# Rotary tables with a longer due time, the decay polynomial in eight late tasks, squares on four regions, the instruction order made anew

## The chip, the cores and the metric

The kernel runs on one core of a Trainium2 chip. The metric is the time of one execution on the device, in microseconds: 1812.16 us is the median of three runs of the kernel before (1810.64 to 1813.06).

## What is computed

One layer of a diffusion backbone on 256 latent and 256 context tokens of width 4096, all in fp32. Modulated RMS-normalised rows go through one wide input projection; its columns are attention queries, keys, values and gate, and the recurrent branch's input and gate. What the change touches is the rotary position code of queries and keys, the RMS norm of each head, and the decay of the recurrence, which needs a softplus of `lam`:

```
mod = silu(c) @ w_ada + b_ada                       # shift, scale, gate
h   = rmsnorm(x, norm_w) * (1 + scale) + shift      # latent rows; context rows likewise
q, k, v, ga, xl, gl = split(h @ w_in)
q, k = rmsnorm per head; q, k = apply_rope(q, k)    # latent rows only
att  = softmax(q k_all) v_all                       # 16 query heads, 4 key heads
u    = short_conv(xl)
r, i = sigmoid(u @ wa + ba), sigmoid(u @ wx + bx)   # block-diagonal
log_a = -8 * r * softplus(-lam)                     # the decay
a, b  = exp(log_a), sqrt(-expm1(2 log_a)) * i * u   # scanned in both directions
out = x + gate * (concat(rmsnorm(att) * silu(ga), rmsnorm(lru) * silu(gl)) @ w_out)
```

## The kernel before, in words

The products run on TensorE in three passes, a weight and an activation each being split into a high part (ScalarE, line 654 for weights) and a low part (VectorE, line 658). Weights come in 512 KB loads from the SP queue (line 305) into six slots; a slot is free again when its low part is made, and the next load is issued then. There are three slots for high parts and three for low parts.

Stage 1 goes over the 32 blocks of 128 input rows in groups of 1, 1, 2, 2, 2 and then 4 blocks. For each group the modulation (w_ada) is computed first, partly on TensorE (line 493), partly on VectorE (481, 483), the activations are scaled, turned and split (605, 615, 616, 625), and then the columns of k, v and the four parts of xl are multiplied (755 to 757). The four tiles of tokens of one column block fill the four PSUM banks `pm`; VectorE adds each to its sum in SBUF (775), which frees the bank for the next column block. Groups go through the six column blocks forwards and backwards in turn, so the last group begins with k. Stage 2 makes the queries (941 to 943), the attention and, beside it, the recurrence; stage 3 the gates (965 to 967); stage 4 the output projection. The gate columns of w_ada are multiplied on VectorE (871, 873) wherever there is room from the end of stage 1 on.

The order of all instructions is made by a planner that runs when the kernel is built (`Plan`, lines 91 to 212). Each `add` gives a task: a function that emits instructions, its costs by engine (P TensorE, A ScalarE, D VectorE, S a transfer issued by GpSimd), the tasks it depends on, a position `pos` (in us of TensorE work) that decides among tasks that can start within 0.10 us of each other, a position `nb` of the main products before which it may not be ordered, and the slots that it takes and gives back. The planner always takes the task that can start earliest. It keeps one clock `dma` for all transfers: a load arrives 1.44 us or more after that clock, and no sooner than 2.2 us after its slot came free (lines 129 to 135); an S task puts its own cost on the same clock:

```
t.end = self.dma = max(self.dma, t.start + 1.3) + t.ops[0][1]   # 205
t.end += 0.9                                                    # 207
```

The order in which tasks are taken is the order of the instructions in each engine's queue; the costs have no other effect.

What the change touches: `decay` (414 to 432) turns `lam` into `lp`, the factor of the decay that the recurrence needs; it is called in one task with `params(1, 2)` at line 830, in the third group. `rope_tasks` (434 to 455) gives two tasks: `load` writes one element on VectorE (440), behind which GpSimd issues eleven transfers (442, 447, 448), and `mul` multiplies the table by the norm's weight (451). It is called for the keys at line 831 and for the queries at line 1417; the keys are normed, rotated and turned in `key_tasks` (1007 to 1045), the queries in `q_head_tasks` (1051 to 1083), and the recurrence's first task depends on the queries' table too (1322). `sum_squares` (979 to 984) squares four heads on ScalarE, each with an accumulator read. `norm_cols` (975 to 977) is a square root on ScalarE and a reciprocal on VectorE.

Of the kernel before, what the change touches and what calls it, by code (L numbers as in the profile page):

```python
# [76 lines left out]
def pe(n, k=1):  # L77
    return k * n / 2400


def mm(n, k=1):

    return k * (n / 2400 + 0.0136)
# [132 lines left out]
def kernel(  # L216
# [197 lines left out]
    def decay():  # L414

        tl = slot("td", [128, 4, 32])
        V.tensor_scalar_mul(tl[:, 0], lam, -1.0)
        V.tensor_tensor(out=tl[:, 1], in0=tl[:, 0], in1=lam, op=ALU.max)
        S.activation(tl[:, 1], tl[:, 1], AF.Exp, scale=-1.0)
        V.tensor_scalar_add(tl[:, 2], tl[:, 1], 2.0)  # L420
        V.reciprocal(out=tl[:, 2], in_=tl[:, 2])
        V.tensor_tensor(out=tl[:, 1], in0=tl[:, 1], in1=tl[:, 2], op=ALU.mult)
        V.tensor_tensor(out=tl[:, 2], in0=tl[:, 1], in1=tl[:, 1], op=ALU.mult)
        V.memset(tl[:, 3], 1.0 / 17.0)
        for k in (15, 13, 11, 9, 7, 5, 3, 1):
            V.tensor_tensor(out=tl[:, 3], in0=tl[:, 3], in1=tl[:, 2], op=ALU.mult)
            V.tensor_scalar_add(tl[:, 3], tl[:, 3], 1.0 / k)
        V.tensor_tensor(out=tl[:, 3], in0=tl[:, 3], in1=tl[:, 1], op=ALU.mult)
        V.tensor_scalar(out=tl[:, 0], in0=tl[:, 0], scalar1=0.0, scalar2=4.0, op0=ALU.max, op1=ALU.mult)
        V.scalar_tensor_tensor(out=lp[:, 0], in0=tl[:, 3], scalar=8.0, in1=tl[:, 0], op0=ALU.mult, op1=ALU.add)  # L430
        V.tensor_scalar_mul(lp[:, 1], lp[:, 0], -1.0)
        drop(tl)

    def rope_tasks(w, pos, after):
# [19 lines left out]
        a = add(load, [("S", 2.0)], after, pos, nb=pos - 20, acq=["u"])  # L454
# [3 lines left out]
    def mod_tasks(k0, nk, out_, p0, p1, nb, cl, on_v=(0, 0)):  # L458
# [58 lines left out]
        for part, col0 in enumerate((128 * k0, D + 128 * k0)):  # L517
# [3 lines left out]
            while k < KT:  # L521
# [8 lines left out]
                else:  # L530
                    m = max(4, step)
                    todo.append(("P", lambda *ws, part=part, k=k: on_tensor(*ws, part=part, k=k), [("P", m // 4 * (pe(4 * n) + 0.2))],
# [139 lines left out]
    def piece(fn, cost, pos, deps, last_of=None, acq=(), rel=()):  # L672


        def run():
            fn()
            if last_of is not None:
                drop(units[last_of]["hi"], units[last_of]["lo"])
            drop(*(x for f in rel for x in f()))

        t = add(run, [("P", cost + 0.025)], [main[0]] + deps, pos, acq=acq, rel=["h4"] * (2 * len(rel)) + (["hi", "lo"] if last_of is not None else []))
        t.main = True
        main[0] = t
        return t
# [145 lines left out]
    t = add(lambda: (params(1, 2), decay()), [("P", 0.3), ("D", 1.0), ("A", 0.3, "exp"), ("D", 2.5)], [p_late], starts[2] - 2, nb=starts[1] + 1, acq=["pe"], rel=["xin", "pe"])  # L830
    k_rope = rope_tasks(k_norm_w, starts[-2] + 8, [t])
# [29 lines left out]
    def gate_tasks(j, prev):  # L861
# [28 lines left out]
        a = add(sums, [("P", 0.43)], [prev], pos, acq=["pe"], rel=["ga"])  # L890
# [315 lines left out]
    def lru_tasks(n, pos, span, prev):  # L1206
# [114 lines left out]
        ld = add(load, [("S", 1.0)], [spilled[n // 4], prev.get("ld")], at(-0.5), nb=at(-0.8), acq=["wg", "xin"])  # L1321
# [9 lines left out]
        for r in range(2):  # L1331
            w = at(0.2 + 0.15 * r)
            ts = []
            for z in range(2):
                a = add(lambda r=r, z=z: gate(r, z), [("P", pe(1536))], [parts], w + 0.06 * span * z, acq=["pe"], rel=["hi", "lo", "lg"] if r and z else [])
# [197 lines left out]
```

## Time and profile before

| | us |
|---|---|
| median of three runs | 1812.16 |
| profiled execution | 1807.69 |
| its span, first to last instruction | 1805.5 |
| TensorE busy (matmul) | 1736.0 |
| VectorE busy | 1383.2 |
| ScalarE busy | 865.0 |
| mean granted TensorE clock | 0.991 |

Times in the profile are counted from the first instruction of the span. PE is TensorE, PEld its weight loads, DVE VectorE, ACT ScalarE, POOL GpSimd, SP SyncE. A wait is written as the instruction that waited, an arrow, and what came last before it could start. Tiles are named as in the program, without buffer numbers: `a` is a sum of stage 1, `hi` and `lo` the parts of a weight, `h` those of the activations, `raw` a load's slot, `rope` and `u` the rotary table and its second factor, `td` the scratch of the polynomial, `ta` and `tp` other scratch.

### The profile page before, as it was taken

The page shows a single profiled execution, that of the slowest core. Times are in us where ns is not written, and L with a number is a line of the kernel's source. Part 1 is how long each engine was busy: PE and PEld are TensorE (multiplying, and loading weights), DVE is VectorE, ACT ScalarE, POOL GpSimd, SP SyncE. Part 2 cuts the span into 40 slices and gives each one's busy share as a digit, 9 for nine tenths or more (in the row PEclk, how much of TensorE's full clock was granted, in tenths as well). Part 3 has the DMA queues.
Part 4 walks back from the last instruction along what each step waited for, and adds up shares of the span by engine and source line. Part 5 has one row for each costly group of instructions (what it writes and reads, how often), then busy time and mean ns, then how long its engine had stood idle before and what let it go on. Part 6 is the DMA issues. An engine that isn't in the chain of part 4 may idle for free.

```text
span 1805.5 us, 25645 instructions
## 1 busy us (share of the span) xinstructions
PE 1736.0 (96%) x9693; PEld 1388.1 (77%) x9693; DVE 1383.2 (77%) x1965; ACT 865.0 (48%) x1282; POOL 67.8 (4%) x111
## 2 busy tenths in 40 slices
PE   3999999999999989999999999999999999999998
PEld 2556667676767767777777889999999988888887
DVE  1278989797978866457789877997996998686864
ACT  5522232232313233347887776868667643333332
POOL 1000000000000010100000000000000000000000
PEclk9999999999999989999999999999999999999999
DMA  9999987869696974863446636875885699898983
GB/s 322 329 303 325 324 302 266 311 227 342 222 345 224 334 198 145 234 195 126 156 148 233 195 110 214 263 232 177 282 268 161 221 322 343 278 334 275 334 273 116
DMA packets 286331, 451.80 MB, mean 250 GB/s; under 512 B 15136, under 2 KB 122512, under 8 KB 285696
## 3 DMA queue, kind: packets, MB, share of 16 engines
q1 hardware_dynamic: 279392, 428.43, 71.1%
q0 software_dynamic: 6816, 21.74, 4.2%
q8 instruction: 76, 1.25, 0.3%
q14 instruction: 47, 0.39, 0.1%
HBM read 441.72 MB, written 8.39 MB: 249 GB/s over the span
## 4 chain that ended last, share of the span: by engine, by line
PE 73%; DVE 14%; DMA 5%; ACT 4%; issue 3%; SPq 1%; POOL 0%; DVEq 0%; ACTq 0%; POOLq 0%
PE pm L755 8%; PE pm L942 8%; PE pm L943 8%; PE pm L941 8%; PE pm L757 7%; PE pm L756 7%; PE pm L965 6%; PE pm L966 6%; PE pm L967 6%; DVE lo L658 4%; DMA raw<-in_w_ada_dram 3%; PE pt L493 2%; PE po L493 2%; DVE ga L873 2%; DVE a L775 1%
## 5 line engine op out<-in xcount | busy, mean ns | idle before, releaser
L654 ACT CAST hi<-raw 128x1024 fp32r<-128x1024 f32 x416 | 436.0, 1049 | 713.2 <-PE pm L757 269.2
L658 DVE TENSOR_TENSOR lo<-raw,hi 128x1024 fp32r<-128x1024 f32 x416 | 506.4, 1220 | 191.3 <-ACT hi L654 189.4
L755 PE MATMUL pm<-hi,h 128*128 128x512 f32 x768 | 318.0, 414 | 16.4 <-DVE a L775 10.9
L941 PE MATMUL pm<-hi,h 128*128 128x512 f32 x768 | 310.2, 404 | 0.0
L942 PE MATMUL pm<-lo,h 128*128 128x512 f32 x768 | 300.1, 391 | 8.0 <-DVE lo L658 8.0
L757 PE MATMUL pm<-hi,h 128*128 128x512 f32 x768 | 302.9, 394 | 3.7 <-DVE h L625 3.7
L756 PE MATMUL pm<-lo,h 128*128 128x512 f32 x768 | 302.8, 394 | 0.8 <-DVE lo L658 0.8
L943 PE MATMUL pm<-hi,h 128*128 128x512 f32 x768 | 300.1, 391 | 0.0
L965 PE MATMUL pm<-h,hi 128*128 128x256 f32 x1024 | 293.7, 287 | 0.0
L967 PE MATMUL pm<-h,lo 128*128 128x256 f32 x1024 | 289.9, 283 | 0.3 <-DVE lo L658 0.3
L966 PE MATMUL pm<-h,hi 128*128 128x256 f32 x1024 | 289.7, 283 | 0.0
L755 PEld LDWEIGHTS pm<-hi,h 128*128 128x128 f32 x768 | 145.6, 190 | 112.6 <-issue 41.4
L965 PEld LDWEIGHTS pm<-h,hi 128*128 128x128 f32 x1024 | 196.2, 192 | 2.2 <-issue 1.2
L966 PEld LDWEIGHTS pm<-h,hi 128*128 128x128 f32 x1024 | 196.3, 192 | 2.1 <-issue 1.2
L967 PEld LDWEIGHTS pm<-h,lo 128*128 128x128 f32 x1024 | 196.2, 192 | 0.5 <-DVE lo L658 0.5
L873 DVE SCALAR_TENSOR_TENSOR ga<-raw,sc,ga 128x512 f32<-128x512 f32 x248 | 185.9, 750 | 10.6 <-DMA raw<-in_w_ada_dram 5.0
L942 PEld LDWEIGHTS pm<-lo,h 128*128 128x128 f32 x768 | 144.8, 189 | 41.2 <-DVE lo L658 9.5
L757 PEld LDWEIGHTS pm<-hi,h 128*128 128x128 f32 x768 | 146.0, 190 | 36.5 <-DVE h L625 4.1
L941 PEld LDWEIGHTS pm<-hi,h 128*128 128x128 f32 x768 | 144.6, 188 | 31.8 <-issue 3.6
L943 PEld LDWEIGHTS pm<-hi,h 128*128 128x128 f32 x768 | 144.4, 188 | 30.6
L756 PEld LDWEIGHTS pm<-lo,h 128*128 128x128 f32 x768 | 146.2, 190 | 27.0 <-DVE lo L658 1.3
L775 DVE TENSOR_TENSOR a<-pm,a 128x512 f32<-128x512 f32 x202 | 132.6, 683 | 32.4 <-PE pm L757 32.1
(193 smaller groups left out, 1710.4 us busy)
## 6 DMA issues: line engine op xcount, KB each, us to landing
raw<-in_w_ada_dram SPq DMA_DIRECT2D x384, 512.0 KB, 5.6
raw<-in_w_in_dram SPq DMA_DIRECT2D x288, 512.0 KB, 4.6
raw<-in_w_out_dram SPq DMA_DIRECT2D x128, 512.0 KB, 5.2
h<-in_x_dram SPq DMA_DIRECT2D x8, 512.0 KB, 9.2
h<-in_ctx_dram SPq DMA_DIRECT2D x8, 512.0 KB, 10.6
xl_d<-a POOLq DMA_DIRECT2D x4, 1024.0 KB, 6.5
xin<-xl_d POOLq DMA_DIRECT2D x16, 256.0 KB, 4.9
a<-in_x_dram POOLq DMA_DIRECT2D x8, 512.0 KB, 7.1
```

Of the source, the lines that this page charges most:

```text
L654: S.copy(d["hi"], raw)
L658: V.tensor_tensor(out=d["lo"], in0=d["raw"], in1=d["hi"].bitcast(F32), op=ALU.subtract)
L755: T.matmul(ps[s, t], hi, wh, start=f, stop=False)
L756: T.matmul(ps[s, t], hi, wl, start=False, stop=False)
L757: T.matmul(ps[s, t], lo, wh, start=False, stop=e)
L873: V.scalar_tensor_tensor(out=d["acc"], in0=w[:, i], scalar=s_, in1=d["acc"], op0=ALU.mult, op1=ALU.add)
L941: T.matmul(ps[t], hi, wh, start=f, stop=False)
L942: T.matmul(ps[t], hi, wl, start=False, stop=False)
L943: T.matmul(ps[t], lo, wh, start=False, stop=e)
L965: T.matmul(o, wh, hi, start=f, stop=False, skip_group_check=True)
L966: T.matmul(o, wh, lo, start=False, stop=False, skip_group_check=True)
L967: T.matmul(o, wl, hi, start=False, stop=e, skip_group_check=True)
```

## The change

The rotary load's cost goes from 2.0 to 15.0 and its `pos` from that of the product to 20 ahead of it; its `nb` is as before, 20 ahead of the product. The keys' call moves from 8 to 28 behind the start of the last group, so that the load may be ordered from 8 behind that start on, and not from 12 ahead of it. The queries' call is as before. `decay` becomes eight tasks in a chain, of which the first may be ordered from 28 behind the start of the last group on; its scratch is a `tp` slot and no longer `td`, and the recurrence's loads wait for the last of the eight in the plan. The squares of four heads go to four regions of one `ta` tile, where each took and gave back the same region. Planned costs of several task kinds are changed (main products, modulation products, squares, gate sums, the recurrence's gates), and the order of the whole kernel is made from them.

```diff
 def mm(n, k=1):
-    return k * (n / 2400 + 0.0136)
+    return k * (n / 2400 + 0.0134)
...
-    def decay():
+    def decay_tasks(pos, step, after):
+        d = {}
+        def begin():
+            tl = d["tl"] = slot("tp", [128, 4, 32])
+            V.tensor_scalar_mul(tl[:, 0], lam, -1.0)
+            V.tensor_tensor(out=tl[:, 1], in0=tl[:, 0], in1=lam, op=ALU.max)
+        def expo():
+            S.activation(d["tl"][:, 1], d["tl"][:, 1], AF.Exp, scale=-1.0)
+        def ratio():
...
+        def series(ks):
+            tl = d["tl"]
+            for k in ks:
+                V.tensor_tensor(out=tl[:, 3], in0=tl[:, 3], in1=tl[:, 2], op=ALU.mult)
+                V.tensor_scalar_add(tl[:, 3], tl[:, 3], 1.0 / k)
+        def finish():
...
+        parts = [(begin, ("D", 0.35)), (expo, ("A", 0.15, "exp")), (ratio, ("D", 1.1))]
+        parts += [(lambda ks=ks: series(ks), ("D", 0.9)) for ks in ((15, 13), (11, 9), (7, 5), (3, 1))] + [(finish, ("D", 0.85))]
+        a = after
+        for i, (fn, op) in enumerate(parts):
+            a = add(fn, [op], [a], pos + step * i, nb=pos - 2 if i == 0 else None, acq=["tp"] if i == 0 else [], rel=["tp"] if fn is finish else [])
+        return a
...
-        a = add(load, [("S", 2.0)], after, pos, nb=pos - 20, acq=["u"])
+        a = add(load, [("S", 15.0)], after, pos - 20, nb=pos - 20, acq=["u"])
         return add(mul, [("D", dve(512))], [a], pos, rel=["u"])
...
-[("P", m // 4 * (pe(4 * n) + 0.2))]
+[("P", m // 4 * (pe(4 * n) + 0.145) + 0.09)]
...
-        t = add(run, [("P", cost + 0.025)], ...
+        t = add(run, [("P", cost)], ...
...
-    t = add(lambda: (params(1, 2), decay()), [("P", 0.3), ("D", 1.0), ("A", 0.3, "exp"), ("D", 2.5)], [p_late], starts[2] - 2, ...
-    k_rope = rope_tasks(k_norm_w, starts[-2] + 8, [t])
+    t = add(lambda: params(1, 2), [("P", 0.37), ("D", 0.9)], [p_late], starts[2] - 2, ...
+    k_rope = rope_tasks(k_norm_w, starts[-2] + 28, [t])
+    decayed = decay_tasks(starts[-2] + 30, 3.0, t)
...
-        a = add(sums, [("P", 0.43)], [prev], pos, acq=["pe"], rel=["ga"])
+        a = add(sums, [("P", 0.8)], [prev], pos, acq=["pe"], rel=["ga"])
...
     def sum_squares(src, ss):
+        j = slot("ta", [128, 4, 128])
         for n in range(4):
-            j = slot("ta", [128, 128])
-            S.activation(j, src[:, n], AF.Square, accum_out=ss[:, n : n + 1])
-            drop(j)
-    SUMSQ = 4 * (act(128) + 0.09)
+            S.activation(j[:, n], src[:, n], AF.Square, accum_out=ss[:, n : n + 1])
+        drop(j)
+    SUMSQ = 4 * (0.215 + 0.091)
...
-        ld = add(load, [("S", 1.0)], [spilled[n // 4], prev.get("ld")], ...
+        ld = add(load, [("S", 1.0)], [spilled[n // 4], prev.get("ld"), decayed], ...
...
-[("P", pe(1536))]
+[("P", 0.693)]
```

## Rows read from the trace of the kernel before

**Rows 1.** The page: busy us (share of the span) and instructions.
```profile
PE 1736.0 (96%) x9693; PEld 1388.1 (77%) x9693; DVE 1383.2 (77%) x1965; ACT 865.0 (48%) x1282; POOL 67.8 (4%) x111
```

**Rows 2.** Waits of PE: waiting line, releaser: us in total, times, longest.
```profile
PE pm L755 <- DVE a L775: 10.9, 4, 8.4
PE pm L942 <- DVE lo L658: 8.0, 2, 7.5
...
PE pm L757 <- DVE h L625: 3.7, 1, 3.7
...
PE pt L493 <- DMA raw<-in_w_ada_dram: 1.7, 3, 1.1
```

**Rows 3.** Windows, early groups: length, busy by engine, PEclk, DMA share, GB/s.
```profile
110.70:116.40 5.70, 5.70 (x24) 2.62 (x24) 2.97 (x6) 0.00 (x0) 0.00 (x0) 0.50 0.92 301
110.00:140.00 30.00, 29.25 (x173) 17.59 (x173) 24.54 (x48) 4.07 (x6) 0.00 (x0) 0.89 0.88 288
140.00:200.00 60.00, 58.56 (x315) 36.34 (x315) 49.22 (x81) 13.25 (x21) 0.00 (x0) 1.00 0.95 330
```

**Rows 4.** Windows, same columns: behind the two long waits, and the last group.
```profile
663.70:669.30 5.60, 5.60 (x15) 4.52 (x16) 5.37 (x9) 4.59 (x9) 0.00 (x0) 0.50 0.37 111
696.00:742.00 46.00, 44.67 (x197) 37.05 (x198) 32.86 (x51) 8.92 (x9) 1.62 (x3) 1.00 0.59 195
...
771.60:775.10 3.50, 3.48 (x10) 2.89 (x11) 2.24 (x2) 0.08 (x1) 0.50 (x1) 0.50 0.90 276
```

**Rows 5.** Timeline of DVE at the polynomial: start, us, line, op, tiles.
```profile
102.59 0.17 DVE L417 TENSOR_SCALAR td<-parT 128x32 f32<-128x32 f32 x1
...
108.98 0.18 DVE L431 TENSOR_SCALAR lp<-lp 128x32 f32<-128x32 f32 x1
...
110.21 0.76 DVE L625 TENSOR_TENSOR h<-ta,h 128x256 fp32r<-128x256 f32 x2
```

**Rows 6.** Timeline of DVE at the keys' rotary table; in brackets, idle before.
```profile
650.98 0.06 DVE L440 MEMSET rope<- 128x1 f32 x1
...
662.33 0.69 DVE L451 TENSOR_TENSOR rope<-rope,u 128x512 f32<-128x512 f32 x1 [11.28 <-DMA u<-in_shape_consts_dram]
```

**Rows 7.** Timeline of DVE in the last group's first column block.
```profile
680.43 1.23 DVE L658 TENSOR_TENSOR lo<-raw,hi 128x1024 fp32r<-128x1024 f32 x1 [4.21 <-ACT hi L654]
681.58 1.28 DVE L775 TENSOR_TENSOR a<-pm,a 128x512 f32<-128x512 f32 x2
```

**Rows 8.** Timeline of SP: issues of loads; two single ones left out.
```profile
647.46 1.50 SPq L305 DMA_DIRECT2D raw<-in_w_in_dram  x2
665.45 0.37 SPq L305 DMA_DIRECT2D raw<-in_w_ada_dram  x1
...
671.45 17.49 SPq L305 DMA_DIRECT2D raw<-in_w_in_dram  x6
```

**Rows 9.** Timeline of DVE at the queries' rotary table.
```profile
757.49 0.06 DVE L440 MEMSET rope<- 128x1 f32 x1
769.74 0.69 DVE L451 TENSOR_TENSOR rope<-rope,u 128x512 f32<-128x512 f32 x1 [12.19 <-DMA wg<-in_lru_wa_dram]
```

**Rows 10.** Timeline of ACT at the keys' squares and their root.
```profile
685.96 0.18 ACT L983 ACTIVATION_READ_ACCUMULATOR ta<-a 128x1 f32 x1
686.17 0.31 ACT L983 ACTIVATE ta<-a 128x128 f32<-128x128 f32 x1
...
693.62 1.28 ACT L976 ACT_TABLE_LOAD   x1
694.92 0.31 ACT L976 ACTIVATE ss<-ss,epsc 128x16 f32<-128x16 f32 x1
```

**Rows 11.** Timeline of ACT at the row statistics, which alternate between two slots.
```profile
41.20 0.20 ACT L392 ACTIVATION_READ_ACCUMULATOR tp<-h 128x1 f32 x1
41.30 0.63 ACT L392 ACTIVATE tp<-h 128x512 f32<-128x512 f32 x1
```

**Rows 12.** Timeline of PE behind the keys' reciprocal.
```profile
697.33 0.47 PE L755 MATMUL pm<-hi,h 128*128 128x512 f32 x1 [1.70 <-DVE a L775]
```

More of the change, by code (lines that the diff above doesn't have):

```diff
@@ L412, in params @@
             V.tensor_scalar_mul(parT[:, 1, 0:32], parT[:, 1, 0:32], 0.5)
-    def decay():
[L416 to L432, printed above, removed]
+    def decay_tasks(pos, step, after):
[8 more added lines that the diff above has]
+            tl = d["tl"]
+            V.tensor_scalar_add(tl[:, 2], tl[:, 1], 2.0)
+            V.reciprocal(out=tl[:, 2], in_=tl[:, 2])
+            V.tensor_tensor(out=tl[:, 1], in0=tl[:, 1], in1=tl[:, 2], op=ALU.mult)
+            V.tensor_tensor(out=tl[:, 2], in0=tl[:, 1], in1=tl[:, 1], op=ALU.mult)
+            V.memset(tl[:, 3], 1.0 / 17.0)
+        def series(ks):
+            tl = d["tl"]
+            for k in ks:
+                V.tensor_tensor(out=tl[:, 3], in0=tl[:, 3], in1=tl[:, 2], op=ALU.mult)
+                V.tensor_scalar_add(tl[:, 3], tl[:, 3], 1.0 / k)
+        def finish():
+            tl = d["tl"]
+            V.tensor_tensor(out=tl[:, 3], in0=tl[:, 3], in1=tl[:, 1], op=ALU.mult)
+            V.tensor_scalar(out=tl[:, 0], in0=tl[:, 0], scalar1=0.0, scalar2=4.0, op0=ALU.max, op1=ALU.mult)
+            V.scalar_tensor_tensor(out=lp[:, 0], in0=tl[:, 3], scalar=8.0, in1=tl[:, 0], op0=ALU.mult, op1=ALU.add)
+            V.tensor_scalar_mul(lp[:, 1], lp[:, 0], -1.0)
+            drop(tl)
+        parts = [(begin, ("D", 0.35)), (expo, ("A", 0.15, "exp")), (ratio, ("D", 1.1))]
[4 more added lines that the diff above has]
+        return a
@@ L679, in run @@
             drop(*(x for f in rel for x in f()))
-        t = add(run, [("P", cost + 0.025)], [main[0]] + deps, pos, acq=acq, rel=["h4"] * (2 * len(rel)) + (["hi", "lo"] if last_of is not None else []))
+        t = add(run, [("P", cost)], [main[0]] + deps, pos, acq=acq, rel=["h4"] * (2 * len(rel)) + (["hi", "lo"] if last_of is not None else []))
         t.main = True
@@ L829 @@
     p_late = add(load_params, [("S", 0.3)], [t], U1 * 0.6)
-    t = add(lambda: (params(1, 2), decay()), [("P", 0.3), ("D", 1.0), ("A", 0.3, "exp"), ("D", 2.5)], [p_late], starts[2] - 2, nb=starts[1] + 1, acq=["pe"], rel=["xin", "pe"])
-    k_rope = rope_tasks(k_norm_w, starts[-2] + 8, [t])
+    t = add(lambda: params(1, 2), [("P", 0.37), ("D", 0.9)], [p_late], starts[2] - 2, nb=starts[1] + 1, acq=["pe"], rel=["xin", "pe"])
+    k_rope = rope_tasks(k_norm_w, starts[-2] + 28, [t])
+    decayed = decay_tasks(starts[-2] + 30, 3.0, t)
     spans = {}
@@ L1319, in at @@
             return pos + span * f
-        ld = add(load, [("S", 1.0)], [spilled[n // 4], prev.get("ld")], at(-0.5), nb=at(-0.8), acq=["wg", "xin"])
+        ld = add(load, [("S", 1.0)], [spilled[n // 4], prev.get("ld"), decayed], at(-0.5), nb=at(-0.8), acq=["wg", "xin"])
         a = add(turn, [("P", 0.44)], [ld, prev.get("cv"), q_rope], at(-0.05), nb=at(-0.6), acq=["pe"], rel=["xin"])
@@ L1334, in lru_tasks @@
             for z in range(2):
-                a = add(lambda r=r, z=z: gate(r, z), [("P", pe(1536))], [parts], w + 0.06 * span * z, acq=["pe"], rel=["hi", "lo", "lg"] if r and z else [])
+                a = add(lambda r=r, z=z: gate(r, z), [("P", 0.693)], [parts], w + 0.06 * span * z, acq=["pe"], rel=["hi", "lo", "lg"] if r and z else [])
                 ts.append(add(lambda r=r, z=z: th(r, z), [("A", act(512) + 0.05, "exp")], [a] + this[:1], w + span * (0.03 + 0.06 * z),
```

2 lines of the change are left out of this document (1 added, 1 removed).

## Prediction

> **What bounds the kernel now.** I read the busy times first: TensorE works for 1736.0 of 1805.5 us [rows 1], so only the 69 us in which it stands, and the stretches in which it runs at half clock, can be won. Then I read TensorE's waits [rows 2]. Most of the rest of the 69 us is the start of the kernel, which the change does not touch. Three long waits are left: 8.4 us on an accumulation (L775), 7.5 us on a low part (L658) and 3.7 us on a remainder of the activations (L625). The windows [rows 3, 4] show that each is followed by TensorE at the lower of its two clock levels (PEclk 0.50): 5.7 us after the first in time, 5.6 and 3.5 us after the others. Work done at half clock takes twice as long, so half of each stretch is lost. The prices are 3.7 + 2.85 = 6.5 us at 107 us, 8.4 + 2.8 = 11.2 us at 655 us and 7.5 + 1.75 = 9.3 us at 764 us, 27 us in all. None of the three is TensorE's own work; in each, VectorE's queue stands still or is busy with something small while TensorE needs the next entry of it.
>
> **Part 1: the decay polynomial leaves the early groups.** Its 27 small VectorE instructions run from 102.59 to 109.16 us, 6.5 us; the remainder that TensorE waits for (L625) is queued right behind them and a low part, at 110.21 [rows 5]. That is the 3.7 us wait, and 2.85 us of half clock follow. Taken away, the low part comes 6.5 us sooner and the wait goes: at most 6.5 us. What is late next are the weight loads: there the transfers run at 330 GB/s when TensorE keeps going (140 to 200 us) and at 288 GB/s over 110 to 140 us [rows 3]. The hole is (330 - 288) x 30 / 330 = 3.8 us of transfers; TensorE cannot get further ahead than the loads do. Bounds 0 (the loads were just in time anyway) and 6.5; I take 3.8, since the windows are the row of that very resource.
>
> **Part 2: the same polynomial in the last group.** The same 6.5 us of VectorE, in eight tasks of at most 1.1 us that other work can stand between. They start 28 us of TensorE work into the last group. From 696 to 742 us VectorE is busy for 32.86 of 46 us [rows 4], so 13.1 us are free and 6.5 fit. Bounds 0 and 6.5 + 2.85 = 9.35 (all of it on the path, as at 102 us); I take 0.5, because the free time is twice what is needed. ScalarE gets an Exp between the keys' Sqrt and the first query head's Sqrt. The table load ahead of the keys' Sqrt (1.28 us at 693.62 [rows 10]) goes, since the last table before it is then a Sqrt's, and one Exp and one Sqrt load come behind it. ScalarE is busy for 8.92 of those 46 us [rows 4]: nothing, at worst 1.3 us. The Sqrt behind the load at 693.62 starts 0.02 us after that load's end [rows 10]. The Trainium skill speaks against the change here: its page "ScalarE: Activation LUTs" (What ACT_TABLE_LOAD costs, and Table sets) wants the functions of one set done together and puts a switch at about 2.66 us, 1.38 of them a drain behind the load. The row shows no such drain; by the page the worst case of this step, and with it the sum, would come out 1.4 us later.
>
> **Part 3: squares without the shared scratch.** In before each square and its accumulator read write one region; the next square starts 0.21 us after the read's start [rows 10]. The row statistics, which alternate between two slots, start 0.10 us after [rows 11]. So 0.11 us go from each of 48 squares. The 32 of the query heads lie in ScalarE's idle time. The 16 of the keys hold the Sqrt, the reciprocal behind it on VectorE, and behind that an accumulation for which TensorE waits 1.70 us at 697.33 [rows 12]. 16 x 0.11 + 1.28 for the table load = 3.0 us sooner is more than 1.70, so this wait closes: bounds 0 and 1.7, I take 1.5.
>
> **Part 4: the keys' rotary table.** Loading it is a VectorE memset (L440), eleven transfers issued by GpSimd behind it, and the product (L451) on VectorE. In before memset and product are neighbours in VectorE's queue: the product stands 11.28 us [rows 6], and all accumulations behind it with it. The change starts the transfer 20 us later than before (8 us into the last group instead of 12 us ahead of it), with a due time 13 us longer. But the planner has one clock for transfers. Line 205 puts the 15 us on that clock, every later weight load is counted from it (lines 130 to 135), and the product is due 1.05 us after it, ahead of the next load's 1.5. So nothing that needs a later load can come between memset and product; only accumulations can. And that clock runs behind: a load's slot comes free six loads before its use. The unit whose low part is at 680.43 [rows 7] was loaded by the second issue of the row at 647.46, six issues before the slot that this low part frees [rows 8]. With 2.2 + 1.44 us for the planner's load the clock stands at 652.2, and 681.6 less the 11.2 us of stall between them is 670.4: it lags by 18 us. 15 + 1.05 us do not make up for 18, so the product is due at once, or after one accumulation. At 8 us into the last group two of the first block's four accumulations are due (the row at 681.58 [rows 7]); the other two then stand behind the product. VectorE stays held for 11.3 us and TensorE again waits for a bank, about 7.7 to 8.4 us, with half clock behind it. The gain is between -1 us (block boundary hit worse) and 9.9 (all accumulations ahead, 1.3 us of wait left, no clock drop). I take 1.0, as the lag of 18 is nearest to the first.
>
> **Part 5: the queries' rotary table.** Position and start are unchanged. VectorE's memset is at 757.49 and the product waits 12.19 us [rows 9] (the name in that row is of the transfer issued behind). By the same rule only VectorE work without loads could come between, and in before there is none at that place although all of it was free to go there: the next entries are low parts [rows 2]. So the 9.3 us stay: bounds of the gain 0 and 9.3, I take 0.
>
> **Part 6: the order made anew.** Planned costs change by 0.02 to 0.37 us a task. I take 0 for it, with 2 us either way: the sum of TensorE's small waits on VectorE that such shifts move is of that size [rows 2].
>
> **Sum.** The profiled execution took 1807.69 us (span 1805.5 and 2.2 around it). 1807.69 - 3.8 + 0.5 - 1.5 - 1.0 - 0 = 1801.9 us. The median of the runs is 1812.16, 4.5 above the profiled one; so 1806.4 us.
>
> **Rivals.** A, the keys' product behind all accumulations: if the planner's clock lags by under 13 us instead of 18, the three open accumulations come first, and TensorE loses about 1.9 us there instead of 10.2: 1806.4 - 8.3 = 1798.1 us. For it: in steady state loads are used faster than in the stretch that I counted. Against: the count. B, the change does what it says, both products find their tables: 1806.4 - 10.2 - 9.3 = 1786.9 us. Against it is line 205. The Trainium skill, page "GPSIMD Engine Reference" (Specifications), adds that GpSimd shares its SBUF interfaces with VectorE instructions of two inputs; no run shown here has both at work during these transfers, and by it they would take longer under cover, not shorter. C, the loads swallow the early gain (TensorE waits for loads of w_ada in places already, 1.7 us of them on L493 alone [rows 2], and each load is as late as its slot comes free): 1806.4 + 3.8 = 1810.2 us, no change. D, slower: hold and decay now fall in one group. 11.3 + 6.5 = 17.8 us against 13.1 free. If the order puts the polynomial ahead of accumulations, VectorE falls 4.7 us behind, the 6.5 us come on the path and the clock falls once more: 4.7 + 6.5 + 2.85 - 0.5 = 13.6, 1820 us. It decides from the point at which the eight pieces, with the wait of the third for Exp, no longer find 6.5 us. Against: TensorE itself stands for most of the hold, so only some 3 us of it become arrears.
>
> **How the numbers follow.** Forecast 0.50, A 0.15, B 0.07, C 0.16, D 0.12. The forecast's own bounds are 1803 to 1810. From 1795 to 1814 only B and D are left out, 0.19. A measurement of this kernel can tell about 0.2%, 3.6 us, from no change. Below 1808.5 lie three quarters of the forecast, A and B: 0.59. Above 1815.8 lies D: 0.12. The rest is 0.29.
>
> **What would show it.** Right: no half clock between 100 and 125 us and no wait of TensorE on L625 there; a wait of the keys' product of about 10 us on VectorE in the last group with a TensorE wait of 7 to 9 us on L775 behind it; a wait of about 7.5 us on a low part at the queries' product; no wait over 1 us at the keys' reciprocal. Wrong: either product without a wait, transfers at 340 GB/s and TensorE waiting for loads from 110 us on, or a new half clock while the polynomial runs.

## The result and the profile after

| | before | after |
|---|---|---|
| median of four runs (us) | 1811.4 | 1787.31 |
| ratio, 95% interval | | 0.9865, 0.9847 to 0.9883 |
| profiled execution, its span (us) | 1807.69, 1805.5 | 1786.01, 1783.9 |
| mean granted TensorE clock | 0.991 | 0.995 |

The change takes 24.1 us away, 1.35%. The time is 19.1 us below the forecast (1806.4) and below its range. All lines of the file behind the new functions stand some 20 lower: L755 to L757 are now L776 to L778, L775 is L796, L942 is L964, L658 is L679, L493 is L514, the rotary memset and product L461 and L472.

The page's busy times after, to be read beside [rows 1]:

```profile
PE 1729.4 (97%) x9693; PEld 1387.2 (78%) x9693; DVE 1383.1 (78%) x1965; ACT 862.4 (48%) x1282; POOL 67.9 (4%) x111
```

VectorE does the same work; TensorE's busy time itself is 6.6 us shorter, with the same 9693 matmuls. Some 4 us of it are half clock, which the prediction had priced; the rest is a surprise, since it had said that only the time in which TensorE stands, and half clock, could be won.

Waits of PE after (waiting line, releaser: us in total, times, longest), beside [rows 2]:

```profile
PE po L514 <- DMA raw<-in_w_ada_dram: 24.9, 13, 18.2
PE pm L776 <- DVE a L796: 7.0, 3, 6.1
PE pm L964 <- DVE lo L679: 4.6, 2, 4.2
...
PE pm L963 <- ACT hi L675: 1.7, 1, 1.7
```

Two of the three long waits are still there, shorter: 6.1 us at the keys' table, 4.2 and 1.7 us at the queries'. The third, on a remainder of the activations, is gone. Windows after (length, busy of PE, PEld, DVE, ACT, POOL, PEclk, DMA share, GB/s), beside [rows 3, 4]:

```profile
104.00:110.00 6.00, 6.00 (x46) 3.80 (x42) 3.19 (x4) 2.66 (x5) 0.00 (x0) 1.00 1.06 353
110.00:140.00 30.00, 29.93 (x192) 18.40 (x184) 24.46 (x47) 4.57 (x5) 0.00 (x0) 1.00 0.98 318
140.00:200.00 60.00, 59.00 (x319) 37.14 (x319) 49.97 (x82) 16.98 (x28) 0.00 (x0) 1.00 0.98 339
670.10:676.90 6.80, 5.91 (x14) 4.67 (x15) 5.27 (x8) 2.54 (x10) 0.00 (x0) 0.50 0.46 141
...
686.00:732.00 46.00, 46.00 (x204) 38.09 (x203) 33.30 (x66) 12.03 (x12) 2.15 (x4) 1.00 0.65 221
...
752.00:758.85 6.85, 3.19 (x8) 2.52 (x9) 5.04 (x6) 0.85 (x1) 2.16 (x3) 0.50 0.54 182
```

In the early groups TensorE runs at full clock and almost without a hole (1.0 of 60 us in the third row). The half-clock stretches (PEclk 0.50) behind the two rotary tables remain. In the fifth row, while the polynomial runs (690.79 to 699.24), TensorE is busy for all 46 us.

Of the 21.6 us of span, the records give 15.0 to TensorE's idle time up to its last matmul (64.7 to 49.7 us), 4.4 to half clock (half of the time worked in it: 10.6 to 6.2), and 2.2 to matmuls that follow each other more closely. By place: about 1.0 at the kernel's start, where the profiled execution of before was 1 us later than those of most kernels here; 6.5 at the early polynomial; 2.2 and 1.8 at the two tables; 1.7 at the keys' reciprocal; the other 8.4 are spread over small waits of all stages. These are places, not yet causes.

### The profile page after: what moved, and what is told of

It is laid out like the page before. It is cut to its first block, busy times and chain, and to the rows that moved or that the text cites. A ratio compares the mean times of both kernels' runs of the same rounds, so it can differ in the third digit from the quotient of the medians.

```text
span 1783.9 us, 25648 instructions
## 1 busy us (share of the span) xinstructions
PE 1729.4 (97%) x9693; PEld 1387.2 (78%) x9693; DVE 1383.1 (78%) x1965; ACT 862.4 (48%) x1282; POOL 67.9 (4%) x111
## 4 chain that ended last, share of the span: by engine, by line
PE 73%; DVE 12%; DMA 7%; ACT 4%; issue 3%; SPq 1%; POOL 0%; DVEq 0%; ACTq 0%; POOLq 0%
PE pm L776 8%; PE pm L964 8%; PE pm L963 8%; PE pm L965 8%; PE pm L777 7%; PE pm L778 7%; PE pm L989 5%; PE pm L987 5%; PE pm L988 5%; DMA raw<-in_w_ada_dram 4%; DVE lo L679 4%; PE pt L514 2%; PE po L514 2%; ACT hi L675 1%; DVE xin L504 1%
## 5 line engine op out<-in xcount | busy, mean ns | idle before, releaser
L679 DVE TENSOR_TENSOR lo<-raw,hi 128x1024 fp32r<-128x1024 f32 x416 | 505.8, 1220 | 185.9 <-ACT hi L675 183.1
L776 PE MATMUL pm<-hi,h 128*128 128x512 f32 x768 | 317.2, 413 | 11.5 <-DVE a L796 7.0
L964 PE MATMUL pm<-lo,h 128*128 128x512 f32 x768 | 300.1, 391 | 4.6 <-DVE lo L679 4.6
L778 PE MATMUL pm<-hi,h 128*128 128x512 f32 x768 | 302.2, 394 | 0.0
L776 PEld LDWEIGHTS pm<-hi,h 128*128 128x128 f32 x768 | 145.6, 190 | 105.5 <-issue 42.5
L964 PEld LDWEIGHTS pm<-lo,h 128*128 128x128 f32 x768 | 144.8, 188 | 36.7 <-DVE lo L679 6.3
L778 PEld LDWEIGHTS pm<-hi,h 128*128 128x128 f32 x768 | 145.7, 190 | 32.4
L796 DVE TENSOR_TENSOR a<-pm,a 128x512 f32<-128x512 f32 x202 | 132.9, 683 | 34.3 <-PE pm L778 34.2
## 6 DMA issues: line engine op xcount, KB each, us to landing
h<-in_ctx_dram SPq DMA_DIRECT2D x8, 512.0 KB, 11.2
```

The lines of the kernel that those rows point to most:

```text
L679: V.tensor_tensor(out=d["lo"], in0=d["raw"], in1=d["hi"].bitcast(F32), op=ALU.subtract)
L776: T.matmul(ps[s, t], hi, wh, start=f, stop=False)
L778: T.matmul(ps[s, t], lo, wh, start=False, stop=e)
L964: T.matmul(ps[t], hi, wl, start=False, stop=False)
```

## Experiments

Medians of three rounds each; the kernel before took 1809.68, 1808.71, 1807.79, 1808.72 and 1810.0 us beside them, in the order of the groups below.

### One part at a time, on the kernel before

`e1_costs`: only the planned costs, six in all, no instruction added or removed:

```diff
-    return k * (n / 2400 + 0.0136)
+    return k * (n / 2400 + 0.0134)
...
-[("P", m // 4 * (pe(4 * n) + 0.2))]
+[("P", m // 4 * (pe(4 * n) + 0.145) + 0.09)]
...
-        t = add(run, [("P", cost + 0.025)], ...
+        t = add(run, [("P", cost)], ...
...
-        a = add(sums, [("P", 0.43)], ...
+        a = add(sums, [("P", 0.8)], ...
...
-    SUMSQ = 4 * (act(128) + 0.09)
+    SUMSQ = 4 * (0.215 + 0.091)
...
-[("P", pe(1536))]
+[("P", 0.693)]
```

> The kernel before with the six planned costs of the change and nothing else; only the order of instructions can differ. Theory O (the new order by itself brings what the sum left out): 8 to 12 us faster than the kernel before, spread over the modulation groups and the attention stage, with the waits at both rotary products as before (8.4 and 7.5 us of TensorE). Rival P (the edits each bring their part and the order nothing): within 2 us of the kernel before.

Measured: 1797.41 us, 0.993 (0.9913 to 0.9947). The order alone is worth 12 us, where the prediction had 0 with 2 either way. At the two tables TensorE stands 9.5 and 7.0 us, so the holds are still there, as theory O had it.

`e2_decay`: only the polynomial in eight late tasks.

```diff
-    t = add(lambda: (params(1, 2), decay()), [("P", 0.3), ("D", 1.0), ("A", 0.3, "exp"), ("D", 2.5)], ...
+    t = add(lambda: params(1, 2), [("P", 0.37), ("D", 0.9)], ...
...
+    decayed = decay_tasks(starts[-2] + 30, 3.0, t)
```

> The kernel before with the decay polynomial in eight tasks in the last group and nothing else. Both theories: the 3.7 us wait of TensorE near 107 us and the half clock behind it are gone. Theory O: 6 to 9 us faster, as the third input block of the changed kernel is reached that much earlier. Rival P (the polynomial's place explains all of the early gain): 10 us or more. By the sum of the prediction: 3.3 us.

Measured: 1807.57 us, 0.9992 (0.9981 to 1.0004): nothing that stands clear of no change, where both theories had 6 us or more. Locally it does what was forecast and more: after 72 of the 768 L755 products TensorE is 9.7 us ahead of before, and it does not stall at the late pieces. But after 288 products 2.1 us are left of that, and the waits of TensorE's weight loads for w_ada between 150 and 590 us rise from 13.0 to 18.7 us (table below). This is what rival C said: the loads swallow the early gain.

`e3_rope`: only the rotary edit.

```diff
-        a = add(load, [("S", 2.0)], after, pos, nb=pos - 20, acq=["u"])
+        a = add(load, [("S", 15.0)], after, pos - 20, nb=pos - 20, acq=["u"])
...
-    k_rope = rope_tasks(k_norm_w, starts[-2] + 8, [t])
+    k_rope = rope_tasks(k_norm_w, starts[-2] + 28, [t])
```

> The kernel before with the rotary loads' cost 15, the new position and the keys' call 20 later, and nothing else. Theory O: 1 to 5 us faster, both products still hold VectorE for 9 us or more. Rival B (the change does what it says): 18 to 21 us faster, no wait at either product.

Measured: 1805.31 us, 0.997 (0.9957 to 0.9984). TensorE still stands 8.65 us at the keys' table, and 1.85 + 4.81 at the queries'.

`e4_squares`: only `sum_squares` with four regions, with its planned cost.

```diff
+        j = slot("ta", [128, 4, 128])
         for n in range(4):
-            j = slot("ta", [128, 128])
-            S.activation(j, src[:, n], AF.Square, accum_out=ss[:, n : n + 1])
-            drop(j)
-    SUMSQ = 4 * (act(128) + 0.09)
+            S.activation(j[:, n], src[:, n], AF.Square, accum_out=ss[:, n : n + 1])
+        drop(j)
+    SUMSQ = 4 * (0.215 + 0.091)
```

> The kernel before with the squares on four regions and their planned cost. Theory O and rival P alike: 0 to 3 us faster; 0.29 us a square instead of 0.43 among the keys', and the 1.7 us wait of TensorE behind the keys' reciprocal is gone.

Measured: 1804.47 us, 0.9966 (0.9954 to 0.9977), about 5 us, where the prediction had 1.5 for the squares. No theory had more than 3. The remainder may again be order, since the planned cost of the squares changes with it; it was not taken apart, and the profiled execution is only 1.5 us shorter than that of before. In its trace the 1.7 us wait is gone and a square starts 0.09 us behind the read before it (0.21 before).

### One part undone, in the kernel after

`f1_early` puts the polynomial back into the third group, `f2_oldcosts` five of the six old costs (all but that of the squares), `f3_norope` the old rotary tasks: the diffs of `e2_decay`, `e1_costs` and `e3_rope` the other way round, as here in `f3_norope`:

```diff
-        a = add(load, [("S", 15.0)], after, pos - 20, nb=pos - 20, acq=["u"])
+        a = add(load, [("S", 2.0)], after, pos, nb=pos - 20, acq=["u"])
...
-    k_rope = rope_tasks(k_norm_w, starts[-2] + 28, [t])
+    k_rope = rope_tasks(k_norm_w, starts[-2] + 8, [t])
```

> The changed kernel with the decay polynomial back in the third group, all else as changed. Alone, the polynomial's move was worth 2 us (0.9992). Theory K (the gain near 107 us is kept only in the new order): 5 to 8 us slower than the changed kernel, ratio to the kernel before about 0.990. Rival S (edits add up): 2 us slower, ratio about 0.9877.

> The changed kernel with the old planned costs of main products, modulation products, gate sums and the recurrence's gates; the three edits stay. Theory O (the new costs' order is half of the gain): 10 to 14 us slower than the changed kernel, ratio to the kernel before 0.992 to 0.995. Rival (the edits carry it): within 3 us of the changed kernel.

> The changed kernel with the rotary loads' cost, position and the keys' call as before. If the products' holds are nearly the same in both (reading of the two traces: 6.1 and 4.2 us of idle TensorE left of 8.4 and 7.5): 3 to 6 us slower than the changed kernel, ratio about 0.989. If the longer due time hides the transfers: 18 us slower.

Measured: 1791.25 us, 0.9909 (0.9892 to 0.9926); 1803.4 us, 0.9972 (0.9959 to 0.9984); 1788.73 us, 0.9895 (0.9879 to 0.9912). Without the new costs three quarters of the gain are gone, although polynomial, rotary edit and squares are all in; that is more than theory O had said (0.992 to 0.995). The polynomial and the rotary edit are worth about 0.4 and 0.3% here, each with an interval of some 0.25.

`g1_later`: does rival B's mechanism exist? The transfer keeps its early place, but takes little of the planner's transfer clock, and the product may not be ordered before its own position:

```diff
-        a = add(load, [("S", 15.0)], after, pos - 20, nb=pos - 20, acq=["u"])
-        return add(mul, [("D", dve(512))], [a], pos, rel=["u"])
+        a = add(load, [("S", 2.0)], after, pos - 20, nb=pos - 20, acq=["u"])
+        return add(mul, [("D", dve(512))], [a], pos, nb=pos, rel=["u"])
```

> The changed kernel with the rotary loads' cost back at 2.0, so that the planner's transfer clock is not pushed, and each product barred from the order until the main products have come 20 us further than at its load. This puts accumulations and low parts between transfer and product. Theory of the hold (the one transfer clock kept product and memset together): no wait over 1 us at either product, no half clock near 670 and 752 us, 9 to 12 us faster than the changed kernel, ratio 0.980 to 0.9815. Rival (something else is late there next): within 4 us of the changed kernel.

Measured: 1770.4 us, 0.9792 (0.9776 to 0.9808), some 13 us better than the change. VectorE's timeline at both tables (start, us, line, op, tiles):

```profile
660.30 0.06 DVE L461 MEMSET rope<- 128x1 f32 x1
...
680.29 1.23 DVE L679 TENSOR_TENSOR lo<-raw,hi 128x1024 fp32r<-128x1024 f32 x1 [1.90 <-ACT hi L675]
681.43 0.68 DVE L472 TENSOR_TENSOR rope<-rope,u 128x512 f32<-128x512 f32 x1
...
733.60 0.06 DVE L461 MEMSET rope<- 128x1 f32 x1
...
752.85 1.23 DVE L679 TENSOR_TENSOR lo<-raw,hi 128x1024 fp32r<-128x1024 f32 x1 [1.50 <-ACT hi L675]
753.99 0.68 DVE L472 TENSOR_TENSOR rope<-rope,u 128x512 f32<-128x512 f32 x1
```

Low parts now stand between memset and product, over 20 us apart, and neither product has an idle bracket. The windows around them show TensorE without a hole and at full clock:

```profile
655.00:690.00 35.00, 35.00 (x156) 29.01 (x155) 25.72 (x48) 12.61 (x41) 6.42 (x12) 1.00 0.63 159
720.00:765.00 45.00, 45.00 (x209) 37.08 (x209) 23.19 (x24) 21.65 (x36) 10.19 (x17) 1.00 0.89 255
```

### Which planned cost it is

All in the kernel after: `h1_oldpiece` puts back the main products' cost alone (0.0136 per matmul and 0.025 per piece), `h2_oldmod` that of the modulation products, `h3_oldgates` those of the gate sums and the recurrence's gates; `h4_cost2` gives the rotary load its old 2.0, at its new place. Of `h1_oldpiece`:

```diff
-    return k * (n / 2400 + 0.0134)
+    return k * (n / 2400 + 0.0136)
...
-        t = add(run, [("P", cost)], ...
+        t = add(run, [("P", cost + 0.025)], ...
```

and of `h4_cost2`:

```diff
-        a = add(load, [("S", 15.0)], after, pos - 20, nb=pos - 20, acq=["u"])
+        a = add(load, [("S", 2.0)], after, pos - 20, nb=pos - 20, acq=["u"])
```

> The changed kernel with the old planned cost of the main products alone (0.0136 a product and 0.025 a piece more). These are 768 of the planner's tasks in stage 1 and half of its TensorE time. Theory M (the main products' planned time, 1.5% too long before, let the order drift against the loads): 10 to 19 us slower than the changed kernel, as with all old costs; ratio 0.992 to 0.997. Rival (the modulation products' cost does it): within 4 us of the changed kernel.

> The changed kernel with the old planned cost of the modulation products alone (0.035 us a task less at 4 rows of a group). Theory M: within 4 us of the changed kernel, ratio 0.985 to 0.989. Rival: 10 us slower or more, with the waits of TensorE for loads of w_ada between 150 and 340 us that the kernel with all old costs has.

> The changed kernel with the old planned costs of the gate sums and of the recurrence's gates alone. Both theories: stage 1 as in the changed kernel until the last group; within 3 us of the changed kernel. Rival (the attention stage's gain comes from these): 3 to 5 us slower, all of it between the second block of query columns and the gates' stage.

> The changed kernel with the rotary loads' planned cost back at 2.0; positions stay. Theory of the one clock (15 on it does not part memset and product by load-dependent work): the same holds, TensorE idle 6 to 8.5 us at the keys' product, 4 to 7.5 at the queries'; within 4 us of the changed kernel, ratio 0.985 to 0.9885. Rival (the 15 is what shortens the holds): 6 us slower or more.

Measured: `h1_oldpiece` 1809.28 us, 1.0002 (0.9993 to 1.0012); `h2_oldmod` 1783.59 us, 0.9864 (0.9844 to 0.9883); `h3_oldgates` 1779.35 us, 0.9852 (0.9827 to 0.9876); `h4_cost2` 1788.58 us, 0.9895 (0.9878 to 0.9913). One cost, that of the main products with its 0.025 us in each piece, carries the whole gain: with the old value the changed kernel is no faster than before, which is more than theory M had said (0.992 to 0.997). (The expectation speaks of 768 tasks; stage 1 has 768 products on L776 in 408 tasks.) Beside the new main cost the other costs make no difference that stands clear of the intervals. Beside the old one they do: `f2_oldcosts` (0.9972), which has three more of them old, is faster than `h1_oldpiece`, and no rule was found for that. 15.0 against 2.0 is worth about 0.3%, with an interval of some 0.25, a little more than was expected. With 2.0 memset and product are neighbours again at both tables, and TensorE stands 8.7 and 7.1 us there; so in this order the 15.0 does shorten the holds, by some 2.6 and 1.2 us.

### Lucky order, or a rule

`i1_mainonly` gives the kernel before the new main-product cost and nothing else:

```diff
-    return k * (n / 2400 + 0.0136)
+    return k * (n / 2400 + 0.0134)
...
-        t = add(run, [("P", cost + 0.025)], ...
+        t = add(run, [("P", cost)], ...
```

`i2_half` and `i3_minus` are the kernel after with half of the excess and with a shortage (`cost - 0.0125`); `i4_later_oldpiece` is `g1_later` with the edit of `h1_oldpiece`.

```diff
-        t = add(run, [("P", cost)], ...
+        t = add(run, [("P", cost + 0.0125)], ...
```

> The kernel before with one edit: the main products' planned cost as the change has it (0.0134 per matmul and no 0.025 us per piece). Theory S (a plan whose main products are longer than the chip's falls behind the chip, and the loads ordered by it come late): this edit alone gives most of what the six planned costs together gave (0.993), so 0.990 to 0.995, about 1794 to 1800 us, and fewer waits of TensorE on loads of w_ada between 150 and 340 us. Theory C (each order is a draw, and the gain of the change is one lucky draw): no such tie, anywhere from 0.985 to 1.005, and as likely over 0.997 as under.

> The changed kernel with half of the planned excess put back: 0.0125 us per piece where the kernel before has 0.025 and the changed one 0. Theory S: between the two, about 0.993 (0.990 to 0.997; 1790 to 1802 us), since the lag of the plan grows with the excess. Theory C: no order in the three; 0.980 to 1.003, as likely outside the two ends as between.

> The changed kernel with its main products planned 0.0125 us per piece too short. Theory S: no lag is left to take away, since the matmuls' pitch on the chip (227 ns) is the planned one already; within 0.5% of the changed kernel (0.982 to 0.991), and no new waits of TensorE on loads between 150 and 340 us. Theory C: 0.980 to 1.003, a loss of over 0.5% as likely as not.

> The kernel with both rotary products parted from their loads in the plan (0.979) with the old planned cost of the main products. Theory S: the two effects lie in different stretches and add, so the 21 us lost by the old cost come back on top: 0.979 + 0.0137 = 0.993, 1791 to 1799 us, still with no wait over 2 us at either product. Theory C: the holds' part (13 us) stays out, since it is a mechanism, but the rest is drawn anew: 0.975 to 0.995.

Measured: 1787.36 us, 0.9885 (0.9863 to 0.9906); 1792.6 us, 0.9912 (0.9893 to 0.993); 1783.2 us, 0.9857 (0.9834 to 0.988); 1789.41 us, 0.9896 (0.9875 to 0.9916). The one cost alone gives the kernel before 21 us, so nearly the whole of what the change brought; what the three edits and the other costs add to it is not clear of the intervals. It is 9 us more than the six costs together brought. Much of that stands at the keys' table: in `i1_mainonly` a low part and two remainders came between memset and product, and TensorE waits 3.4 us there, against 9.5 in `e1_costs` and 8.4 in before. So some of the 21 us is this one place, which the other pairs share less or not at all.

Half of the excess lies between none and all of it, a shortage costs nothing in sum, and in the kernel without rotary holds the old cost takes 19 us again. Two of the four fall into theory S's range, two outside it to the fast side (`i1_mainonly` under 0.990, `i4_later_oldpiece` under 1791 us); the directions are all as it said. Theory C, a lucky draw, allowed each of them by itself. Against it stands the whole set: without the edit of `g1_later`, the six kernels with the full excess lie at 0.9966 to 1.0002 and the eight without it at 0.9852 to 0.993; with that edit, at 0.9896 and at 0.9763 to 0.9792.

What the excess does in stage 1 is seen in the waits that neither [rows 1] nor [rows 2] show: those of TensorE's weight loads (PEld) in the modulation products. There w_ada is the moving operand, but the wait for its transfer stands mostly at the load of the stationary one, which comes first. From 150 to 590 us, before, `h1_oldpiece` and `i1_mainonly`:

```profile
PEld po L493 <- DMA raw<-in_w_ada_dram: 7.4, 9, 1.7
PEld pt L493 <- DMA raw<-in_w_ada_dram: 5.6, 8, 2.0
...
PE pt L493 <- DMA raw<-in_w_ada_dram: 1.7, 3, 1.1
PE po L493 <- DMA raw<-in_w_ada_dram: 1.5, 4, 0.8
```

```profile
PEld pt L514 <- DMA raw<-in_w_ada_dram: 10.6, 13, 1.8
PEld po L514 <- DMA raw<-in_w_ada_dram: 8.7, 8, 2.5
...
PE po L514 <- DMA raw<-in_w_ada_dram: 3.1, 4, 1.6
...
PE pt L514 <- DMA raw<-in_w_ada_dram: 2.2, 4, 0.9
```

```profile
PEld pt L493 <- DMA raw<-in_w_ada_dram: 2.6, 4, 0.8
PEld po L493 <- DMA raw<-in_w_ada_dram: 2.4, 4, 1.2
...
PE po L493 <- DMA raw<-in_w_ada_dram: 0.5, 2, 0.3
```

PEld waits for w_ada 13.0, 19.3 and 5.0 us in these three. The waits of PE, 3.2, 5.3 and 0.5 us, are the same time seen again: they lie inside those of PEld, and the rest of PEld's passes under a running matmul. A second number is free of such doubts: the time from the start of one modulation matmul to the start of the next, between the 72nd and the 576th product on L755 (L776), all such steps added (434 to 469 of them; L493 and L506, in the longer files L514 and L527). Kernels whose instructions have the same order in that stretch share a row:

| excess per piece (us) | kernels | PEld's wait for w_ada, 150 to 590 us | from modulation matmul to the next, us |
|---|---|---|---|
| 0.025 | before, `e3_rope`, `e4_squares` | 13.0, 14.3, 17.2 | 44.9, 46.1, 45.5 |
| 0.025 | `e2_decay`, `f2_oldcosts` | 18.7, 23.3 | 48.8, 53.5 |
| 0.025 | `h1_oldpiece`, `i4_later_oldpiece` | 19.3, 17.5 | 52.0, 50.2 |
| 0.0125 | `i2_half` | 9.2 | 40.9 |
| 0 | after, `f3_norope`, `g1_later`, `h3_oldgates`, `h4_cost2`, `j1_later_gates` | 9.4, 10.9, 11.8, 7.1, 9.0, 14.2 | 40.8, 41.7, 41.9, 38.3, 40.5, 42.9 |
| 0 | `e1_costs`, `f1_early` | 7.3, 5.5 | 40.2, 39.0 |
| 0 | `h2_oldmod`, `j2_later_gates_mod` | 4.3, 8.7 | 37.6, 41.4 |
| 0 | `i1_mainonly` | 5.0 | 35.0 |
| -0.0125 | `i3_minus` | 5.4 | 40.6 |

One and the same order waits between 7.1 and 14.2 us for w_ada from kernel to kernel, so single waits say little; but the last column parts the kernels without overlap, 44.9 to 53.5 us with the full excess and 35.0 to 42.9 without. Three pairs differ by that cost alone. Their steps among modulation matmuls differ by 9.9 (before and `i1_mainonly`), 11.2 (`h1_oldpiece` and after) and 8.3 us (`i4_later_oldpiece` and `g1_later`), and the whole stretch by 8.7, 8.3 and 8.5. So the loss of this stretch stands at the modulation products. The pairs are not three independent draws: `i4_later_oldpiece` has in stage 1 the order of `h1_oldpiece`, and `g1_later` that of after.

Part of PEld's wait is booked as TensorE's busy time: the modulation products of the form 128x512 into `po` (line, op, tiles, shapes, count | busy, mean ns | idle before), before and `i1_mainonly`,

```profile
L493 PE MATMUL po<-raw,wg 128*32 128x512 f32 x216 | 35.5, 605 | 1.5 <-DMA raw<-in_w_ada_dram 1.5
```

```profile
L493 PE MATMUL po<-raw,wg 128*32 128x512 f32 x216 | 31.9, 604 | 0.5 <-DMA raw<-in_w_ada_dram 0.5
```

are booked with the same 605 and 604 ns each, and together take 3.6 us less: they overlap more, so some of the waiting, booked at the weight loads ahead of them, had stood in the busy time.

The excess can be set beside the chip. In the window from 686 to 732 us of after, shown above, TensorE does nothing but main products; 208 of them in a row start 226.76 ns apart in the records. A piece of six is 6 x (512/2400 + 0.0134) = 1.360 us in the new plan, 6 x 0.22676 = 1.361 on the chip, and 6 x (512/2400 + 0.0136) + 0.025 = 1.387 in the old plan, 1.9% over the undisturbed pitch. Stage 1 has 408 pieces (48 in the two groups of one block, 360 in the others), so the 0.025 us come to 10.2 us of planned time there.

That the old plan thereby falls behind the chip, as theory S says, is not borne out. The times that the planner itself gives to its tasks are, from the 72nd to the 576th product on L755 (L776), 427.8 us for before, 431.6 for `h1_oldpiece`, 422.8 for `i1_mainonly` and 425.6 for after; the chip takes 449.9, 454.9, 441.2 and 446.6. The old plan, too, is shorter than the chip. And the pieces are not always undisturbed: behind other work the second matmul of a piece starts 0.33 us after the first and not 0.23 (some 84 times in that stretch, before and after alike, about 9 us in all). Why the longer planned piece places the modulation products worse among the loads stays open.

Stage 1 is not the whole of it either. By the start of stage 2 `h1_oldpiece` is 13.4 us behind after (part of it at the keys' table, where TensorE waits 8.7 and 6.1 us) and `i4_later_oldpiece` 11.2 behind `g1_later`; by the end of the span it is 20.6 and 19.7. The later stages have main products with the same cost, and what the excess does there was not looked into. `i2_half` loses nothing against after up to the 576th product (0.4 us); its 6.1 us stand at the keys' table (8.7 us of waiting) and behind it.

### A version better than both

`j1_later_gates` is `g1_later` with the old costs of gate sums and recurrence gates, `j2_later_gates_mod` the same with the old cost of the modulation products too. Of the former:

```diff
-        a = add(sums, [("P", 0.8)], ...
+        a = add(sums, [("P", 0.43)], ...
...
-[("P", 0.693)]
+[("P", pe(1536))]
```

> The kernel with both rotary products parted from their loads in the plan (0.9792) and the old planned costs of the gate sums and of the recurrence's gates, which alone took the changed kernel from 0.9865 to 0.9852. If the parts add, 0.978, about 1768 us; if the small edits are draws, 0.976 to 0.983.

> As the other of this pair, with the old planned cost of the modulation products as well (alone 0.9864, no change against 0.9865). If the parts add, 0.978, about 1768 us, within 0.2% of the other; if the small edits are draws, 0.976 to 0.983.

Measured: 1767.6 us, 0.9763 (0.9738 to 0.9787), and 1768.25 us, 0.9768 (0.9746 to 0.9791). Both beat the changed kernel by about 1%, most of it by the parting of load and product (0.7); against `g1_later` the intervals overlap.

## Why the prediction was wrong, point by point

**What bounds the kernel.** The premise was that only the 69 us of standing and the half clock could be won. It led past the modulation products: I looked at PE's waits, where L493 waits 1.7 us for `pt` [rows 2], and left out the row for `po`,

```profile
PE po L493 <- DMA raw<-in_w_ada_dram: 26.5, 14, 19.3
```

of which 19.3 us are the start of the kernel and 7.2 are not; and I did not look at PEld's waits, 13.0 us for the same loads between 150 and 590 us.

**Part 6, the step that failed.** "I take 0 for it, with 2 us either way" stood on the small waits of TensorE on VectorE; the order's effect on the waits for loads was put at nothing. 0.025 us a piece over the 408 pieces of stage 1 could have been multiplied from the diff: 10.2 us of planned time. That this makes TensorE faster needed experiments; that it is no small shift did not. The six costs together measured 12 us (`e1_costs`), the main products' cost alone 21 us (`i1_mainonly`), and without it the change is worth nothing (`h1_oldpiece`). In stage 1 the gain stands at the modulation products; by what step of the planner it comes about stays open.

**Part 1, mis-sized.** The mechanism held: no half clock, no wait on L646 (L625 in before). But the cap of 3.8 us did not hold at that place: it took 330 GB/s [rows 3] for all that the transfers can do, and the windows after show 353, 318 and 339 GB/s (339 in the same sum would give 4.5 us). Between the 48th and the 72nd main product the kernel after gains 6.1 us on before, near the upper bound of 6.5. Then the lead melts: of the 6.2 us by which after leads `f1_early` at the 72nd product, 3.3 are left at the 288th. What the end keeps is nothing clear under the old costs (`e2_decay`), and under the new ones 0.44% by the medians of `f1_early` but only 0.6 us between the profiled executions. Which of the two it is stays open.

**Part 2, right.** No stall while the polynomial runs; the cost is 0, not 0.5.

**Part 3, right.** ScalarE's timeline after, at the keys' squares and their root, to be read beside [rows 10]:

```profile
662.02 0.19 ACT L1005 ACTIVATION_READ_ACCUMULATOR ta<-a 128x1 f32 x1
662.11 0.29 ACT L1005 ACTIVATE ta<-a 128x128 f32<-128x128 f32 x1
...
673.96 1.05 ACT L675 CAST hi<-raw 128x1024 fp32r<-128x1024 f32 x1 [1.64 <-PE pm L778]
674.91 0.30 ACT L998 ACTIVATE ss<-ss,epsc 128x16 f32<-128x16 f32 x1
```

The next square starts 0.09 us behind the read's start (0.21 before, 0.10 forecast), no table load stands ahead of the root, and the 1.70 us wait [rows 12] is gone.

**Part 4, right in its mechanism.** VectorE's timeline after at the keys' table, then TensorE's:

```profile
658.27 0.06 DVE L461 MEMSET rope<- 128x1 f32 x1
659.49 0.69 DVE L796 TENSOR_TENSOR a<-pm,a 128x512 f32<-128x512 f32 x1 [0.56 <-PE pm L778]
669.64 0.69 DVE L472 TENSOR_TENSOR rope<-rope,u 128x512 f32<-128x512 f32 x1 [9.46 <-DMA u<-in_shape_consts_dram]
670.25 0.68 DVE L796 TENSOR_TENSOR a<-pm,a 128x512 f32<-128x512 f32 x1
```

```profile
670.99 0.80 PE L776 MATMUL pm<-hi,h 128*128 128x512 f32 x1 [6.09 <-DVE a L796]
```

One accumulation came between memset and product, one of the two cases that the forecast allowed; the product waits 9.46 us, and the accumulation behind it holds TensorE for 6.09 us (forecast 7.7 to 8.4), with half clock from 670.10 to 676.93. The gain was 2.2 us (forecast 1.0, bounds -1 and 9.9). How many accumulations come between depends on the order: none in `i2_half`, where TensorE waits 8.7 us, and two in `i3_minus`, where it waits 4.7.

**Part 5, right in its mechanism.** At the queries' table after, VectorE and then TensorE:

```profile
741.10 0.06 DVE L461 MEMSET rope<- 128x1 f32 x1
748.76 0.16 DVE L905 TENSOR_TENSOR gT<-pe,parT 128x4 f32<-128x4 f32 x1 [7.60 <-PE pe L901]
...
753.78 0.69 DVE L472 TENSOR_TENSOR rope<-rope,u 128x512 f32<-128x512 f32 x1 [4.72 <-DMA wg<-in_lru_wa_dram]
```

```profile
751.01 0.49 PE L963 MATMUL pm<-hi,h 128*128 128x512 f32 x1 [1.71 <-ACT hi L675]
755.66 0.79 PE L964 MATMUL pm<-lo,h 128*128 128x512 f32 x1 [4.16 <-DVE lo L679]
```

Only work that needs no new load stands between (a gate's last step, which itself waits for TensorE, and a memset on L1435), where the prediction had expected none; the low part that TensorE needs is still behind the product. The hold cost 1.8 us less than before, where 0 was forecast. The rule behind the forecast does not hold in every order: in `e3_rope` a low part did come between at this table, and the product still waits 12.3 us.

**Rivals.** The time came out within 0.4 us of rival B, but not by B: both products still wait. B's mechanism is `g1_later`, and it is worth another 13 us. That fits the line named against it: the 15 us stand on the one transfer clock, and in the change no low part is ordered in between; `g1_later` alters both that cost and the product's bar, and `h4_cost2` shows that the cost alone frees nothing. The transfers do take longer under cover, as the prediction had warned: from memset to the last landing 17.3 and 16.5 us in `g1_later`, against 11.0 and 11.8 in before. Whether VectorE's work or the weight loads beside them cause that is not shown; the 20 us between memset and product cover it. Rival C was true of the order of before (`e2_decay`); for the new one it is open (part 1). D's bunching of hold and polynomial did not come.

## What to carry to other kernels

Where an order is planned from costs, change the planned length of the commonest task first, with its undisturbed pitch in the trace as the mark: 1.9% over that pitch cost more here than three edits aimed at visible stalls brought, and 0.9% under it did no harm. Why is not known, so try it and do not reckon it. Read the waits of TensorE's weight loads as well as its own, since a transfer that is late can be waited for there, and that time be booked as busy. And to hide a transfer issued behind a small instruction, part that instruction and the consumer in the queue by an explicit position; a longer planned duration on a shared transfer clock shortened the holds here by 1 to 3 us and did not end them.

## What the runs showed of the hardware

A stream of main products with 512 moving columns, each with a weight load, starts every 226.76 ns at full clock (208 in a row). The Trainium skill, page "TensorE: Matmul & The Clock Gate" (Back-to-back issue gap), gives about 216 ns for the gap between single matmuls of that width and about 131 ns for a sustained stream with weight loads. For these fp32r products the first is 5% short and the second is not seen; the measurement decides.

The transfers reached 339 GB/s over 60 us with TensorE running, at a busy share of 0.98 (353 over a window of 6 us, at a share of 1.06, owes something to the window's edges); the 330 GB/s that I had taken for their limit were moved at a share of 0.95 [rows 3]. Eleven transfers issued by GpSimd behind one memset took 11.0 to 12.3 us up to the last landing while VectorE stood for most of that time (before and after, both tables), and 16.5 to 17.3 us in `g1_later`, where VectorE worked and weight loads went on. ScalarE's square behind an accumulator read starts 0.09 us after the read's start where both squares write regions of their own, and 0.21 us where they share one.
